# Order of the last three Strassen products of an FFN output, its residual loads, and the order of the MLA projections behind it

## The chip, the cores and the metric

The kernel runs on one core of a Trainium2 chip. The metric is the device time of one execution in microseconds (us), lower is better. The core's engines are named as the profile names them: PE is TensorE (matrix products into PSUM, with PEld for its weight loads), DVE is VectorE, ACT is ScalarE, POOL is GpSimd and SP is SyncE. Loads and stores are issued from the queues of SP, ACT and POOL.

## The reference, cut to what matters

A backbone of two layers runs over 256 latent tokens and 256 context tokens, width 1024. Layer 0 mixes tokens with an mLSTM, layer 1 with multi-head latent attention (MLA); a gated ConvFFN follows each.

```python
x = _layer_norm(ALPHA * x + ml[2] * yl, ln_g[i, 0], ln_b[i, 0])
f = _conv_ffn(_modulate(x, ml[3], ml[4]), ...)
x = _layer_norm(ALPHA * x + ml[5] * f, ln_g[i, 1], ln_b[i, 1])
# the same for the context xc while need_ctx (layer 0 only)

def _conv_ffn(h, w_in, conv_w, conv_b, w_out):
    gate, up = jnp.split(h @ w_in, 2, axis=-1)
    return (jax.nn.silu(_dwconv(gate, conv_w, conv_b)) * up) @ w_out

def _mla_mixer(hl, hc, ...):            # layer 1
    kc, vc = _mla_kv(hc, w_dkv, kv_norm, w_ukv, None)
    kl, vl = _mla_kv(hl, w_dkv, kv_norm, w_ukv, ang)
    ql = _mla_q(hl, w_dq, q_norm, w_uq, ang)
    # latent queries attend to context and latent keys; then @ w_out
```

The change lies between the product with `w_out` of layer 0's FFN ("fout0", 2816 x 1024) and the MLA's keys, values and queries.

## The kernel before

**Arithmetic.** Every float32 matrix product is made of three products of rounded parts (`mm3`: hi x hi, hi x lo, lo x hi). A weight block of 128 x 1024 goes through three steps: a DMA brings it from `in_ws` into a raw tile, ACT rounds it to the high part (L321), and DVE subtracts for the low part (L324). The last two steps are called the split.

**The weight stream.** `_plan` writes the order of all weight blocks out by hand, and the class `Stream` follows it. `use(key)` hands the next block over and splits ahead, at most `NB` = 3 blocks in the "w" buffers; blocks marked wide go to "u" buffers instead and don't count among the three. Raw tiles come from a ring of slots that changes with the stage (`bufs`, L240 to L252): eleven slots from `yt2` on, seven from `y22` on. A slot is loaded again when its block has been split.

**fout0 as one level of Strassen's scheme.** `w_fout0` (L1350) multiplies the FFN's activations, halves of context rows (g = 0) and latent rows (g = 1), with `w_out` in seven products instead of eight. The first four (`yt2`, `y11`, `yt3`, `yt1`, six blocks each, interleaved) fill all eight PSUM banks, a pair for each product: p6, p1, p7, p5. Their sums go to SBUF (`sums`, as a background generator). Then `y21`, `y22` and `yt4` run one after the other, each into a fresh pair of banks. `add` (L1452) multiplies a finished pair by the gate row, adds it to the residual tile `z` and takes the statistics for the layer norm. The weight of `yt4` is a sum: the weight of `yt2`, stored in `t2d`, is loaded back on SP's queue, and the second addend is added by an accumulating load on POOL's queue (L276, L277). The activations of these three products ("zr", then "fz" after their own split) come back from DRAM in 33 loads on ACT's queue (`operand`, L1359).

**Residuals.** Before, `sums` writes gate x partial sum into each half of `z` and adds the residual row `x1d` by an accumulating DMA on POOL's queue (L1424), eight of 256 KB.

**What follows.** When the context rows are complete (after `y22`) they are normalised (`z_norm`), transposed on PE and modulated (`ctx_T`, through `ln_T`) between the two halves of `yt4`'s tail; then the latent rows. `mla_down` (L1609) makes the down projection of the context (`dkv`), the latent transposes, dkv of the latent rows, and the context's keys (`ukn`) and values (`uv`). `mla` makes the query projection `dq`, the latent keys, the rotary queries and the latent values, then attention. `ln_x` scales the latent rows for the next residual and stores them in `x2d`.

**Order.** DVE, ACT, SP and POOL get their order from a planner that takes instructions in program order as their inputs come ready, with `pin` holding some ACT instructions in program order. Each engine then works through its instructions strictly in that order. PE is held in program order from `yt4` on (`manual_schedule`). Background generators (`bg`) are advanced one step at each `tick`.

Of the kernel before, what the change touches and what calls it, by code (L numbers as in the profile page):

```python
# [55 lines left out]
YTAIL = 3  # L56
# [13 lines left out]
def _plan():  # L70
# [162 lines left out]
class Stream:  # L233


    def __init__(self, k, ids, order, ws):
# [14 lines left out]
        self.bufs.append((keys.index(("y22", 0, 0)), self.bufs[-1][1][:7]))  # L251
# [101 lines left out]
class K:  # L353
# [996 lines left out]
    def w_fout0(self, x1d, ctx_T, lat):  # L1350
# [4 lines left out]
        parts = [("2", i) for i in range(6)] + [("S4", i) for i in range(6)] + [("3", i) for i in range(6)]  # L1355
# [20 lines left out]
        def prod(ps, x, w, i, bs=(0, 1)):  # L1376
            for h in range(2 if i < 5 else 1):
                j = 2 * i + h
                a = A[x, j]
                for b in bs:  # L1380
                    ts = slice(b * 128, (b + 1) * 128)
                    cs = slice(h * 512, (h + 1) * 512)
                    self.mm3(ps[b], (a[:, 0, ts], a[:, 1, ts]), (w[0][:, cs], w[1][:, cs]), j == 0, j == 10)
# [7 lines left out]
        u1, u3, u4, vv = [], [], [], []  # L1391
        for i in range(6):
            for name, ps, x in (("yt2", p6, "S2"), ("y11", p1, "1"), ("yt3", p7, "S3"), ("yt1", p5, "S1")):
# [21 lines left out]
        stats = [self.tiny(12, "st").rearrange("p (a b) -> p a b", b=6) for _ in range(4)]  # L1415
        z = [self.uf("z") for _ in range(4)]

        def sums():

            def part(us, g, c):  # L1420
                for b in range(2):
                    zz = z[2 * g + b][:, c]
                    nc.vector.tensor_tensor(zz, us[b], gate[g][:, c], op=ALU.mult)
                    nc.gpsimd.dma_start(zz, x1d[2 * g + b][:, c], accum_op=ALU.add)  # L1424
            for b in range(2):
                u = self.s2("u2")
                nc.vector.tensor_tensor(u, p6[b], u1[b], op=ALU.add)
                u4.append(u)
            yield
            part(u1, 0, lo)  # L1430
            yield
            for b in range(2):
                u = self.s2("u3")
                nc.vector.tensor_tensor(u, p7[b], u4[b], op=ALU.add)
                u3.append(u)
            yield
            for b in range(2):
                v = self.s2("v")
                nc.vector.tensor_tensor(v, p5[b], u3[b], op=ALU.subtract)
                vv.append(v)  # L1440
            yield
            for b in range(2):
                nc.vector.tensor_tensor(u4[b], p5[b], u4[b], op=ALU.subtract)
            yield
            part(u4, 0, hi)
            yield
            part(u3, 1, lo)
            yield
            part(vv, 1, hi)
            yield  # L1450

        def add(g, c, ps, bs=(0, 1)):  # L1452
            for b in bs:
                t = self.s2("zp")
                zz = z[2 * g + b][:, c]
                nc.vector.tensor_tensor(t, ps[b], gate[g][:, c], op=ALU.mult)
                nc.vector.tensor_tensor(zz, zz, t, op=ALU.add)
                nc.vector.bn_stats(stats[2 * g + b][:, c.start // 512], zz)

        self.bg.append(sums())  # L1460
        ps = pair()
        for i in range(6):
            w = st.use(("y21", 0, i))
            prod(ps, "2", w, i)
            self.tick(1)
            operand()
        add(0, lo, ps)
        ps = pair()
        for i in range(6):
            w = st.use(("y22", 0, i))  # L1470
            prod(ps, "S4", w, i)
            self.tick(1)
            operand()
        self.drain()
        add(0, hi, ps)
        self.bg = [self.z_norm(z[0:2], stats[0:2])]
        with self.tc.manual_schedule(engines={mybir.EngineType.PE}):
            ps = pair()
            st.limit = [x[0] for x in st.order].index(("ukn", 0, 0))
            for i in range(6 - YTAIL):  # L1480
                w = st.use(("yt4", 0, i))
                prod(ps, "3", w, i)
                self.tick(1)
                for b in range(2):
                    if i == 2:
                        nc.vector.bn_stats(stats[2 + b][:, 1], z[2 + b][:, hi])
            self.drain()
# [483 lines left out]
```

## Time and profile before

| what | value |
|---|---|
| runs | 1403.27, 1405.13, 1408.07 us; median 1405.13 us |
| profiled execution | 1403.4 us, its span from the first to the last instruction |
| PE busy | 1359.0 us (97%) |
| PEld busy | 1143.8 us (82%) |
| DVE busy | 1070.7 us (76%) |
| ACT busy | 699.4 us (50%) |
| POOL busy | 126.5 us (9%) |
| mean granted clock of TensorE | 0.991 |
| DMA | 297.63 MB, mean 212 GB/s |

Busy shares are means over stages with different limits. PE counts as busy while a matmul is in flight, and matmuls overlap, so its loss shows in three places: idle time with what ended it, the granted clock, and the distance between the starts of successive matmuls. An entry like "[11.88 <-DVE w L324]" says that the engine had been idle for 11.88 us and that the instruction of line 324 on DVE, writing tile w, let it go on.

### The profile page before, as it was taken

How to read it: one execution, taken by the hardware profiler on the slowest of the kernel's cores; microseconds unless marked ns; L12 is line 12 of the kernel's file. 1: busy time of each engine (PE TensorE's matmuls, PEld its weight loads, DVE VectorE, ACT ScalarE, POOL GpSimd, SP SyncE). 2: the span in 40 equal slices, each digit the busy share in tenths (PEclk: the TensorE clock that was granted, in tenths of full speed). 3: DMA queues.
4: the chain of work that ended last, by engine and by line, in shares of the span. 5: the costliest groups of instructions: out<-in, count | busy, mean ns of one | idle time of the engine just before them, and what ended most of it. 6: DMA issues, size and time to landing. Idle time of an engine off the chain costs nothing.

```text
span 1403.4 us, 19160 instructions
## 1 busy us (share of the span) xinstructions
PE 1359.0 (97%) x6903; PEld 1143.8 (82%) x6903; DVE 1070.7 (76%) x1718; ACT 699.4 (50%) x1179; POOL 126.5 (9%) x219
## 2 busy tenths in 40 slices
PE   7999999999999999999999999999968899999997
PEld 3788888888788888878888888888747788999986
DVE  6599756687688697698799887669858789777773
ACT  6585444445544535374553433334527467455560
POOL 0032000010011001110011000000030001000000
PEclk9999999999999999999999999999989999999999
DMA  9689848788665364676747877547894425357650
GB/s 336 222 291 327 282 161 249 238 289 277 212 222 189 109 237 158 202 224 199 260 153 262 278 226 236 168 147 268 257 246 160 149 84 198 125 188 227 209 187 30
DMA packets 98479, 297.63 MB, mean 212 GB/s; under 512 B 12200, under 2 KB 24872, under 8 KB 98384
## 3 DMA queue, kind: packets, MB, share of 16 engines
q1 hardware_dynamic: 68672, 218.52, 47.1%
q0 software_dynamic: 18048, 57.57, 13.5%
q10 hardware_dynamic: 11664, 20.32, 4.0%
q8 instruction: 54, 0.88, 0.3%
q14 instruction: 41, 0.34, 0.1%
HBM read 262.90 MB, written 33.46 MB: 211 GB/s over the span
## 4 chain that ended last, share of the span: by engine, by line
PE 88%; DVE 4%; DMA 3%; ACT 2%; issue 1%; SPq 0%; ACTq 0%; DVEq 0%; POOLq 0%
PE fin L381 9%; PE fin L383 9%; PE fin L382 9%; PE tok L381 6%; PE tok L383 6%; PE tok L382 6%; PE y L382 5%; PE y L383 5%; PE y L381 4%; PE qk L381 4%; PE qk L383 4%; PE qk L382 4%; PE up L381 2%; PE up L383 2%; PE up L382 2%; DMA raw<-in_ws 2%
## 5 line engine op out<-in xcount | busy, mean ns | idle before, releaser
L324 DVE TENSOR_TENSOR w<-raw,w 128x1024 fp32r<-128x1024 f32 (+3 forms) x290 | 348.1, 1203 | 163.0 <-ACT w L321 162.2
L321 ACT CAST w<-raw 128x1024 fp32r<-128x1024 f32 (+3 forms) x290 | 300.3, 1037 | 329.1 <-PE fin L383 106.4
L382 PE MATMUL fin<-h,w 128*128 128x256 f32 (+1 forms) x696 | 231.7, 333 | 0.0
L383 PE MATMUL fin<-h,w 128*128 128x256 f32 (+1 forms) x696 | 231.4, 333 | 0.0
L381 PE MATMUL fin<-h,w 128*128 128x256 f32 (+1 forms) x696 | 231.2, 333 | 0.1
L510 DVE SCALAR_TENSOR_TENSOR junk<-ar,bc 128x1024 f32<-128x1024 f32 x128 | 156.0, 1218 | 4.7 <-ACT bc L552 2.4
L382 PEld LDWEIGHTS fin<-h,w 128*128 128x128 f32 x696 | 132.2, 190 | 13.1 <-DVE h L1210 0.2
L383 PEld LDWEIGHTS fin<-h,w 128*128 128x128 f32 x696 | 132.2, 190 | 12.9
L381 PEld LDWEIGHTS fin<-h,w 128*128 128x128 f32 x696 | 131.9, 190 | 12.9 <-ACT h L1209 0.3
L381 PE MATMUL qk<-xc,w 128*128 128x512 f32 x256 | 100.7, 393 | 0.0
L383 PE MATMUL qk<-xc,w 128*128 128x512 f32 x256 | 99.9, 390 | 0.0
L382 PE MATMUL qk<-xc,w 128*128 128x512 f32 x256 | 99.8, 390 | 0.0
L381 PEld LDWEIGHTS qk<-xc,w 128*128 128x128 f32 x256 | 48.1, 188 | 10.1 <-issue 0.4
L383 PEld LDWEIGHTS qk<-xc,w 128*128 128x128 f32 x256 | 48.1, 188 | 10.0
L382 PEld LDWEIGHTS qk<-xc,w 128*128 128x128 f32 x256 | 48.1, 188 | 9.6
L381 PE MATMUL up<-hT,w 128*128 128x512 f32 x128 | 50.5, 394 | 0.4 <-ACT hT L386 0.3
L382 PE MATMUL up<-hT,w 128*128 128x512 f32 x128 | 50.2, 392 | 0.5 <-DVE hT L387 0.5
L383 PE MATMUL up<-hT,w 128*128 128x512 f32 x128 | 50.1, 391 | 0.3 <-DVE w L387 0.3
L381 PE MATMUL tok<-w,hT 128*128 128x512 f32 x128 | 49.8, 389 | 0.0
L382 PE MATMUL tok<-w,hT 128*128 128x512 f32 x128 | 49.8, 389 | 0.0
L383 PE MATMUL tok<-w,hT 128*128 128x512 f32 x128 | 49.8, 389 | 0.0
L321 ACT CAST wu<-raw 128x1024 fp32r<-128x1024 f32 (+1 forms) x33 | 33.7, 1039 | 23.7 <-DMA raw<-in_ws 23.7
(451 smaller groups left out, 3049.5 us busy)
## 6 DMA issues: line engine op xcount, KB each, us to landing
raw<-in_ws SPq DMA_DIRECT2D x287, 512.0 KB, 4.4
ar<-in_adaT SPq DMA_DIRECT2D x80, 512.0 KB, 4.8
adaw<-in_ada_w SPq DMA_DIRECT2D x32, 256.0 KB, 6.5
t2d<-raw ACTq DMA_DIRECT2D x13, 512.0 KB, 4.6
raw<-t2d SPq DMA_DIRECT2D x13, 512.0 KB, 7.2
raw<-in_ws POOLq DMA_DIRECT2D x13, 512.0 KB, 8.9
zr<-fd ACTq DMA_DIRECT2D x33, 128.0 KB, 4.4
xmd<-xr POOLq DMA_DIRECT2D x16, 256.0 KB, 5.2
```

The lines of the kernel that those rows point to most:

```text
L321: k.nc.scalar.copy(h[:, :cols], src)
L324: k.nc.vector.tensor_sub(l[:, :cols], src, h[:, :cols])
L381: mm(out, w[0], x[0], start=start, stop=False)
L382: mm(out, w[0], x[1], start=False, stop=False)
L383: mm(out, w[1], x[0], start=False, stop=stop)
L510: nc.vector.scalar_tensor_tensor(o, w, 1.0, self.bc[j], op0=ALU.mult, op1=ALU.mult, accum_out=col[:, k, j:j + 1])
```

## The change

1. The last three products run in another order: two blocks of `y21`, all of `yt4`, the rest of `y21`, then `y22`. The latent rows are complete after `yt4`, the context rows after `y22`. The ring of raw slots keeps eleven slots until `yt4` has been loaded.
2. Each of the three accumulates onto a bank pair that is already live: `y21` onto p1, `yt4` onto p7 (into which ACT first copies u3 = p7 + t), `y22` onto p5 (from which t has been subtracted), where t = p6 + u1.
3. The residual rows `x1d` are loaded into `z` by four plain DMAs during the first four products; every `add` then multiplies, adds and takes statistics.
4. Latent rows are normalised and transposed (`lat_T`) between the products of `y22`. PE is held in program order for all three products.
5. `mla_down` runs dkv of the latent rows, then `dq`, then the context transposes, the latent keys and dkv of the context. The context's keys and values come in `mla`, after the rotary queries. The blocks of `dq` come right behind those of `dkv` in the stream and are wide.
6. Keys of two heads share a tile pair and are split once per full PSUM bank.

```diff
-YTAIL = 3
+YTURN = 2
+YLAST = ([("y21", j) for j in range(YTURN)] + [("yt4", j) for j in range(6)] +
+         [("y21", j) for j in range(YTURN, 6)] + [("y22", j) for j in range(6)])
 ...
-    for n in ("y21", "y22", "yt4"):
-        for j in range(6):
-            add((n, 0, j), cols[j], n == "yt4" and j >= 6 - YTAIL)
+    for n, j in YLAST:
+        add((n, 0, j), cols[j])
     for c, m in enumerate((3, 3, 2)):
         add(("dkv", 0, c), m * 320)
+    for c in range(4):
+        add(("dq", 0, c), 768, True)
 ...
-    for c in range(4):
-        add(("dq", 0, c), 768)
 ...
-        self.bufs.append((keys.index(("y22", 0, 0)), self.bufs[-1][1][:7]))
+        self.bufs.append((keys.index(("y21", 0, YTURN)), self.bufs[-1][1][:7]))
 ...
-                if n == 14:
-                    gate = []
-                    for g in (1, 0):
-                        t = self.uf("gate")
-                        nc.gpsimd.dma_start(t, self.gd[0, 5][g:g + 1, :].to_broadcast([128, 1024]))
-                        gate.append(t)
+                if n in (14, 18):
+                    g = 1 - len(gate)
+                    r = self.uf("gate")
+                    nc.gpsimd.dma_start(r, self.gd[0, 5][1 - g:2 - g, :].to_broadcast([128, 1024]))
+                    gate.append(r)
+                    for b in range(2):
+                        z[2 * g + b] = self.uf("z")
+                        nc.gpsimd.dma_start(z[2 * g + b], x1d[2 * g + b])
                 n += 1
                 if (name, i) == ("y11", 5):
                     for b in range(2):
                         u = self.s2("u1")
                         pin(nc.scalar.copy(u, p1[b]))
-                        u1.append(u)
+                        r = self.s2("u2")
+                        nc.vector.tensor_tensor(r, p6[b], u, op=ALU.add)
+                        t.append(r)
+                if (name, i) == ("yt3", 5):
+                    u3 = []
+                    for b in range(2):
+                        r = self.s2("u3")
+                        nc.vector.tensor_tensor(r, p7[b], t[b], op=ALU.add)
+                        nc.scalar.copy(p7[b], r)
+                        u3.append(r)
 ...
-        def sums():
-            def part(us, g, c):
-                for b in range(2):
-                    zz = z[2 * g + b][:, c]
-                    nc.vector.tensor_tensor(zz, us[b], gate[g][:, c], op=ALU.mult)
-                    nc.gpsimd.dma_start(zz, x1d[2 * g + b][:, c], accum_op=ALU.add)
+        for b in range(2):
+            r = self.s2("v")
+            nc.vector.tensor_tensor(r, p5[b], u3[b], op=ALU.subtract)
+            v.append(r)
 ...
+        def latent():
+            yield from add(1, lo, p7)
+            for _ in self.z_norm(z[2:4], stats[2:4]):
+                pass
+            yield
+            yield
+            yield from lat_T(z[2:4])
+
+        def context():
+            yield from add(0, hi, p5)
+            yield from self.z_norm(z[0:2], stats[0:2])
+
+        st.limit = kv0
+        with self.tc.manual_schedule(engines={mybir.EngineType.PE}):
+            for name, i in YLAST:
+                if (name, i) == ("y21", YTURN):
+                    self.drain()
+                    self.bg = [latent()]
+                w = st.use((name, 0, i))
+                ps, more = {"y21": (p1, True), "yt4": (p7, True), "y22": (p5, True)}[name]
+                prod(ps, names[name], w, i, more)
+                if (name, i) == ("yt4", 0):
+                    for b in range(2):
+                        nc.vector.tensor_tensor(p5[b], p5[b], t[b], op=ALU.subtract)
+                    self.bg = [add(1, hi, v)]
+                self.tick(1)
+                operand()
+                if (name, i) == ("y21", 5):
+                    self.bg.append(add(0, lo, p1))
+            self.drain()
+            self.fa = self.fd = None
+            down(context(), z)
 ...
     def ukn(self, g):
-            u = self.kn[h]
-            self.split(u[:, 0, cs], u[:, 1, cs], ps[:, hs])
+            if h % 2:
+                u, v = self.kn[h // 2]
+                self.split(u[:, g], v[:, g], ps)
 ...
+    def mla_down(self, hl, hc, context, ctx_T):
+        wd = [st.use(("dkv", 0, c), hold=True) for c in range(3)]
 ...
+        rows = self.dkv_mm(hl, wd)
+        for _ in context:
+            pass
+        rows = self.dkv_rows(rows, 2)
 ...          # the dq products, as before in mla
+        st.pump(kv0 + 4)
+        self.dkv_T(rows, 2)
 ...          # row norms of dq; wk, wv
+        ctx_T()
+        self.ukn(1)
+        rows = self.dkv_mm(hc, wd)
+        st.unhold("dkv")
+        self.rows = self.dkv_rows(rows, 0)
 ...
     def mla(self):
+        self.uv((2, 3))
 ...          # dq's transposes, rotary query products
         self.drain()
-        self.uv((2, 3))
+        self.dkv_T(self.rows, 0)
+        self.ukn(0)
+        self.uv((0, 1))
```

More of the change, by code (lines that the diff above doesn't have):

```diff
@@ L1348, in act_sums, with w_fout0 @@
         self.fd.append(d)
-    def w_fout0(self, x1d, ctx_T, lat):
+    def w_fout0(self, x1d, kv0, lat_T, down):
         nc, st, A = self.nc, self.st, self.fa
         pin = self.tc.keep_in_program_order
-        parts = [("2", i) for i in range(6)] + [("S4", i) for i in range(6)] + [("3", i) for i in range(6)]
+        names = {"y21": "2", "yt4": "3", "y22": "S4"}
+        parts = [(names[n], i) for n, i in YLAST]
         off = {"2": 0, "3": 256, "S4": 512}
@@ L1390, in w_fout0 @@
         n = 0
[L1391 removed]
+        t, v = [], []
+        z, gate = [None] * 4, []
         for i in range(6):
@@ L1458, in add @@
                 nc.vector.bn_stats(stats[2 * g + b][:, c.start // 512], zz)
[L1460 to L1487, printed above, removed]
-            ws = [(i, st.use(("yt4", 0, i), hold=True)) for i in range(6 - YTAIL, 6)]
-            for b in range(2):
-                for i, w in ws:
-                    prod(ps, "3", w, i, (b,))
-                add(1, lo, ps, (b,))
-                if b == 0:
-                    ctx_T(z[0:2])
-            st.unhold("yt4")
-            self.fa = self.fd = None
+                yield
@@ L1897, in build, with lat_T, down, ctx_T @@
         hc, hl = half(hcu), half(hlu)
-        def ctx_T(zs):
+        def lat_T(zs):
             k.rope_load()
-            for _ in k.ln_T(zs, *k.ln_mod_cols(1, 1, 0, 1), hc, False):
-                pass
-        def lat(zs):
-            def latent():
-                hlu.extend([k.u("hl") for _ in range(4)])
-                for _ in k.ln_T(zs, *k.ln_mod_cols(1, 1, 0, 0), hl, True):
-                    pass
-            k.mla_down(hc, latent, hl)
-            k.late.append(k.ln_x(1, zs, [x2d[0], x2d[1]]))
-        k.w_fout0(x1d, ctx_T, lat)
+            hlu.extend([k.u("hl") for _ in range(4)])
+            yield from k.ln_T(zs, *k.ln_mod_cols(1, 1, 0, 0), hl, False)
+        def down(context, z):
+            def ctx_T():
+                hcu.extend([k.u("hc") for _ in range(4)])
+                for _ in k.ln_T(z[0:2], *k.ln_mod_cols(1, 1, 0, 1), hc, True):
+                    pass
+            k.mla_down(hl, hc, context, ctx_T)
+            k.late.append(k.ln_x(1, z[2:4], [x2d[0], x2d[1]]))
+        k.w_fout0(x1d, kv0, lat_T, down)
         hc = hcu = None
         k.take_late()
-        att = k.mla(hl)
+        att = k.mla()
         oT = next(att)
```

106 lines of the change are left out of this document (36 added, 70 removed).

## The prediction, made before the change was run

> **What bounds the kernel now.** I read the page first, then the span cut into stages, then the waits of TensorE in the stage that the change rewrites, and last the timelines of the engines around its longest wait. The page:
>
> ```profile
> span 1403.4 us, 19160 instructions
> ...
> PEclk9999999999999999999999999999989999999999
> ```
>
> The granted clock leaves the top tenth in one slice, the 30th of 40 (35.1 us each), which lies in the changed stage. The profiled execution takes its span, 1403.4 us; the three timed runs lie between 1403.27 and 1408.07 with median 1405.13. So I work on the profiled span and take the median to be 1.7 us above it, before and after alike. Busy time by stage (columns: stretch, its length, then busy time and count for PE, PEld, DVE, ACT, POOL, then granted clock, DMA share, GB/s):
>
> ```profile
> 941.00:1001.00 60.00, 60.00 (x267) 49.64 (x265) 51.06 (x58) 31.29 (x41) 2.19 (x4) 1.00 0.75 253
> 1001.00:1017.00 16.00, 15.48 (x68) 12.30 (x67) 15.64 (x21) 8.70 (x12) 1.82 (x2) 1.00 0.83 232
> 1017.00:1033.00 16.00, 14.88 (x66) 12.02 (x65) 12.43 (x17) 4.92 (x6) 7.08 (x8) 1.00 1.02 247
> 1033.00:1060.00 27.00, 14.99 (x55) 11.42 (x53) 14.14 (x20) 8.90 (x11) 3.53 (x4) 0.75 0.92 239
> 1060.00:1086.00 26.00, 22.84 (x149) 21.07 (x149) 21.31 (x57) 21.78 (x51) 2.25 (x4) 1.00 0.41 136
> 1086.00:1100.00 14.00, 9.35 (x52) 8.07 (x53) 10.92 (x30) 5.00 (x14) 0.31 (x1) 0.88 0.55 178
> 1100.00:1131.00 31.00, 30.24 (x173) 27.24 (x172) 22.04 (x41) 16.06 (x33) 1.87 (x4) 1.00 0.39 135
> ```
>
> The first row is the four paired products (yt2, y11, yt3, yt1): TensorE never idles there. The next three hold y21, y22 and yt4, the last three the MLA projections up to the first query product. TensorE's idle time is length minus busy: 0.5, 1.1, 12.0, 3.2, 4.7 and 0.8, together 22.2 us. No more than this and some clock is there to be won. TensorE's waits in the six stages after 1001 (us in all, times, the longest):
>
> ```profile
> PE y L382 <- DVE w L324: 13.5, 3, 11.9
> PE kn L381 <- DVE kn L387: 3.8, 4, 1.1
> PE kn L381 <- ACT ckT L1574: 1.8, 2, 1.0
> PE zT L1197 <- DVE z L1512: 1.7, 2, 0.9
> PE kn L382 <- DVE ckT L1575: 0.5, 1, 0.5
> PE dkv L383 <- DVE hl L1210: 0.4, 1, 0.4
> PE dkv L381 <- ACT hl L1209: 0.4, 1, 0.4
> ```
>
> The longest, 11.9 us, is a wait for the split of a yt4 weight on VectorE. What VectorE did then, and TensorE after it:
>
> ```profile
> 1027.74 1.82 DVE L324 TENSOR_TENSOR w<-raw,w 128x1024 fp32r<-128x1024 f32 x2
> 1043.93 0.69 DVE L1486 BATCH_NORM_STATS2 st<-z 128x6 f32<-128x512 f32 x1 [14.37 <-DMA z<-x1d]
> 1044.54 1.21 DVE L324 TENSOR_TENSOR w<-raw,w 128x1024 fp32r<-128x1024 f32 x1
> ```
> ```profile
> 1045.80 0.79 PE L382 MATMUL y<-w,fz 128*128 128x512 f32 x1 [11.88 <-DVE w L324]
> 1046.39 0.63 PE L383 MATMUL y<-w,fz 128*128 128x512 f32 x1
> ...
> 1050.66 0.58 PE L381 MATMUL y<-w,fz 128*128 128x512 f32 x1
> 1051.08 0.39 PE L382 MATMUL y<-w,fz 128*128 128x512 f32 x1
> 1051.31 0.39 PE L383 MATMUL y<-w,fz 128*128 128x512 f32 x1
> ```
>
> So the weight was not what came last. VectorE stood 14.4 us at the statistics of a residual half that an accumulating DMA (z<-x1d) had still to add to, and the weight's split was queued behind. Afterwards ten starts take 4.27 us (0.43 each) until the clock is back, then 0.23: twelve matmuls lost 0.2 us each, 2.4 us. The DMAs of 1001 to 1060 (median us from issue to landing at the end):
>
> ```profile
> raw<-t2d SPq DMA_DIRECT2D x5, 512.0 KB, 9.3
> raw<-in_ws POOLq DMA_DIRECT2D x5, 512.0 KB, 11.9
> z<-x1d POOLq DMA_DIRECT2D x8, 256.0 KB, 12.4
> ```
>
> **The change, part by part.** *Residuals.* Eight accumulating loads of 256 KB go, and with them the statistics' wait: minus 11.9 and minus 2.4 us of clock. In their place stand four plain loads of 512 KB, issued on the POOL queue at products 14 and 18 of the first stage, next to the two gate loads. The gates are the nearest row for them, and the operand loads (zr) are what shares the queues there:
>
> ```profile
> zr<-fd ACTq DMA_DIRECT2D x33, 128.0 KB, 4.4
> ...
> gate<-gd POOLq DMA_DIRECT2D x2, 512.0 KB, 5.6
> ```
>
> At 5.6 us each they land some 20 us before first use, so nothing waits for them. The Trainium skill would price this otherwise: its page "DMA: Bandwidth & Descriptors", section "Anatomy of one DMA — SWDGE (gpsimd) path", fits 2.0 us plus bytes over 436 GB/s, an estimated 2.6 us for 256 KB, at which the accumulating loads would have hindered nobody. The trace's 12.4 us disagrees, and the measurement decides; what the sum would be by that rule stands among the rivals.
>
> What would be late next is yt4 itself: reloaded from t2d on SP, then added to by an accumulating load on POOL. At the medians above that is 21.2 us. yt4's first weight is now the 27th of the order instead of the 37th, inside the ring of eleven raw slots, so it is requested at product 13, thirteen products ahead. A product is twelve starts of 0.23, 2.7 us, four of the thirteen are halves: 30 us, less 2 for the slot's last reader. 28 exceeds 21.2, without the residuals in the queue. How fast accumulation runs, and what it does to others, a stretch shows in which it had the chip:
>
> ```profile
> q0 software_dynamic: 333, 0.97, 103.4%
> q1 hardware_dynamic: 2, 0.00, 0.2%
> ```
>
> This is 1023 to 1029, POOL's queue against SP's: 0.97 MB in 6 us, so 3.2 us for 512 KB and 18 us for the five and a half of yt4; the last lands about when its split is due. SP's loads issued meanwhile moved two packets. Those 18 us now run beside the end of the first stage, whose DMA share is already 0.75, and beside the zr loads on ACT's queue. Their casts stand in program order among ACT's weight casts:
>
> ```profile
> 997.61 0.62 ACT L1371 CAST fz<-zr 128x512 fp32r<-128x512 f32 x1 [1.00 <-DMA zr<-fd]
> ...
> 1000.13 1.06 ACT L321 CAST w<-raw 128x1024 fp32r<-128x1024 f32 x1
> ```
>
> Already now ACT waits 1.0 us for a zr, and the weight cast behind it ends 0.05 us before y21 wants it. A zr pair is requested two products ahead: 5.4 us, but 2.7 us in the last four half products. One accumulation of 3.2 us in front of it delays the casts of perhaps two pairs, less the two split weights in hand: I take 3.0 us, between 0 (ACT's queue shares evenly) and 15 (18 us of accumulation, all but 3 of it felt).
>
> *Product order and live banks.* The six sums p6+u1, p7+t and p5-u3 move from y21 into the last four half products, where VectorE also splits weights. The rows of a full split, of a key split and of a half-width operation (count, busy us, mean ns):
>
> ```profile
> L324 DVE TENSOR_TENSOR w<-raw,w 128x1024 fp32r<-128x1024 f32 x16 | 19.5, 1216 | 2.7 <-ACT w L321 2.7
> ...
> L387 DVE TENSOR_TENSOR kn<-kn 128x256 fp32r<-128x256 f32 x16 | 6.5, 419 | 3.9 <-ACT kn L386 3.9
> ...
> L1456 DVE TENSOR_TENSOR zp<-y,gate 128x512 f32<-128x512 f32 x6 | 4.0, 679 | 0.0
> ```
>
> Six times 0.68 is 4.1 us more within 5.4 us; VectorE idles 15% of the first stage, and the two split weights ahead cover most. I take 1.0 us, from 0 to 4.1. The seeded banks cost TensorE nothing: as many matmuls, and the ACT copies into p7 have two products, 5.4 us, before yt4 needs them. After them the eight gate multiplications become two more of the add's trios: 24 operations where 28 stood, 2.7 us off VectorE, off the path.
>
> *Latent rows first.* Twelve of the sixteen latent transposes go between y22's products. Before the first lie y21's last four products and one of y22, 12.2 us; adding, statistics and normalisation of two rows need about 6 x 0.68 plus 2 us of small steps, beside five splits of 1.2: 12 us. I take 0.3 us of wait, 0 to 3. The waits of zT (1.7) and the two of dkv for hl (0.4 each) go: minus 2.5.
>
> *MLA order.* Context rows now finish behind the latent dkv and dq products. Their lengths, from starts of today's:
>
> ```profile
> 1067.07 0.30 PE L381 MATMUL dkv<-w,hc 128*128 128x320 f32 x1
> ...
> 1074.11 1.91 PE L1197 MATMUL zT<-ident,z 128*128 128x128 f32 x16
> ```
> ```profile
> 1104.54 0.33 PE L381 MATMUL dq<-w,hl 128*128 128x384 f32 x1
> ...
> 1112.89 0.82 PE L1570 MATMUL ckT<-ident,ckr 128*128 128x128 f32 x6
> ```
>
> 7.0 and 8.4, together 15.4 us of cover, against 4.1 for the add, about 4.6 for dq and dkv splits, 2 for the normalisation and 2 for the row norms on VectorE: 12.7, so it holds, with little to spare. If the cover is short, each missing us is one of TensorE. The sixteen key splits become eight over full banks, so TensorE no longer waits for VectorE to read the first half of the bank it writes: minus 3.8, and with it the low clock of that stretch (9.35 us at 0.88, 1.1 us). Here the clock falls after gaps of 1.1 us at most. The Trainium skill's page "TensorE: Matmul & The Clock Gate", section "Part 1: The HAM clock gate", has the clock fall only after an idle window of about 3.4 us; by it these 1.1 us would stay and the gain be smaller by as much. The trace's 0.88 speaks against that. Transposes of context rows now stand between the ckT transposes and the first keys and fill most of kn's waits for ckT (1.8 and 0.5): minus 1.5 of 2.3. Against this, VectorE's work, 96.5 us in the six stages, is squeezed from 130 us into some 113: I take 1.5 us of new waits, 0 to 8. The residual's scaling (eight operations of 0.68, 5.4 us, four loads and four stores on POOL) moves from beside dq to the drain ahead of the context's transposes. Queued behind it on VectorE are the ckT splits that ukn(0) needs; ready value products cover most: 0.5 us, 0 to 5.4.
>
> **Sum.** Off: 11.9 + 2.4 + 2.5 + 3.8 + 1.1 + 1.5 = 23.2. On: 3.0 + 1.0 + 0.3 + 1.5 + 0.5 = 6.3. Net minus 16.9: 1386.5 on the profiled span, 1388.2 as a median.
>
> **Rivals.** *VectorE becomes the bound.* It is at 15.64 of 16 us in the stage after 1001. If splits come late throughout, its terms stand at their upper ends (4.1, 3, 8, 5.4 for 3.3): on is 23.5 with zr's 3.0, the net about 0, 1405; halfway 1397. For: the density; against: a 97% stage now costs 0.5 us. *Slower: ACT stands at zr.* If a pair takes L to land and is asked for two products ahead, ten products from 14 on last L/2 each, against 6 x 2.7 + 4 x 1.36 = 21.6 us. To lose the 19.9 us that are otherwise won, and 4.2 more, L must pass 9.1 us; today it is 4.4. At the 12.4 us of loads behind accumulation the loss is 40 us: about 1425. For: SP's two packets in 6 us; against: accumulation is 18 us in all, and this case takes ten products at 9.1 / 2, 46 us of it. *The wait was not the residuals'*, as by the rule's 2.6 us, or the z tiles find no free slot and load late: 14.3 of the 23.2 stay, net minus 2.6, 1402.5. Against it stands the 14.37 us wait, ended by that very DMA.
>
> **How the numbers follow.** Forecast 0.70; VectorE 0.13, of it half way mostly; zr 0.12; the last 0.05. Something of 0.3%, 4.2 us, is about what a measurement of this kernel can tell from no change. Faster: 0.70 + 0.13 = 0.83; same: 0.05; slower: 0.12. The range's low end is all idle time and clock won, 25.7 off 1405.1: 1379. Its high end, 1400, takes in VectorE's half way case and zr up to 15; above lie zr's case, the last and the tail of VectorE's.
>
> **What would show it.** No row of statistics waiting for z<-x1d; yt4's accumulating loads landing before 1018; every slice of the clock at 9; kn's wait for kn gone; DVE w waits under 3 us together. Step zr is wrong if the operand cast's wait for zr grows past 5 us in all, the projections' step if TensorE idles over 4 us between y22's end and the queries. The forecast falls if y's wait for w stays above 10 us.

## The result, and the profile after

| kernel | median | lowest to highest | ratio to before, 95% interval |
|---|---|---|---|
| before | 1405.14 us | 1403.27 to 1410.52 | |
| changed | 1410.99 us | 1407.69 to 1413.01 | 1.003, 1.0015 to 1.0044 |

The change made the kernel slower by 0.3% where 1.2% faster was forecast. Median and direction both miss, and what came is the rival called slower, though at a smaller price. The profiled execution of the changed kernel took 1407.69 us for a span of 1405.8. A gap of this size stands in every run that was profiled after the change (1.7 to 2.1 us), so it is no difference between runs. The profiled execution is the fastest of the eight: its span is 2.4 us longer than that of before, while the medians differ by 5.9. What the slower executions lost besides, the trace cannot show.

The page of the changed kernel, and the span in the stretches of before (same columns). TensorE idles 0.9 us in the first, then 12.5, 3.0, 0, 2.4, 3.7 and 3.5; the last stretches do not hold quite the same work, since the first query product (tile qn) starts at 1133.62 instead of 1130.86:

```profile
span 1405.8 us, 19141 instructions
...
PEclk9999999999999999999999999999899999999999
```
```profile
941.00:1001.00 60.00, 59.10 (x261) 48.52 (x259) 48.56 (x54) 27.31 (x34) 6.25 (x9) 1.00 0.76 245
1001.00:1017.00 16.00, 3.53 (x12) 2.06 (x11) 4.35 (x7) 5.26 (x9) 3.38 (x5) 0.74 1.06 274
1017.00:1033.00 16.00, 13.04 (x51) 9.77 (x51) 11.92 (x17) 7.58 (x11) 0.00 (x0) 0.94 0.85 287
1033.00:1060.00 27.00, 27.00 (x125) 22.38 (x124) 22.00 (x33) 14.70 (x21) 0.00 (x0) 1.00 0.60 182
1060.00:1086.00 26.00, 23.56 (x136) 21.62 (x134) 21.66 (x37) 15.54 (x28) 0.00 (x0) 1.00 0.59 182
1086.00:1100.00 14.00, 10.28 (x70) 9.95 (x71) 12.60 (x40) 10.58 (x32) 2.20 (x4) 0.76 0.62 188
1100.00:1131.00 31.00, 27.48 (x166) 24.45 (x165) 23.40 (x44) 13.85 (x27) 2.16 (x4) 1.00 0.37 122
```

Two holes have opened. TensorE's waits from 999 to 1134 name them (us in all, times, the longest):

```profile
PE y L1386 <- ACT u L1420: 10.9, 1, 10.9
PE ckT L1550 <- DVE ckr L1503: 5.8, 2, 4.8
PE y L1386 <- DVE w L325: 2.6, 2, 2.3
PE y L1386 <- ACT w L322: 2.5, 2, 1.6
PE kn L383 <- DVE ckT L1555: 2.3, 1, 2.3
PE kn L382 <- ACT ckT L1554: 0.9, 1, 0.9
```

The 11.9 us for the split behind the statistics and the 3.8 us for half key banks are gone, as are the waits for z and hl. In their place TensorE stands 10.9 us at y21's first product, which accumulates onto p1 and so may not start before ACT has copied u1 out of it. What ACT did then, from its timeline, and TensorE after it:

```profile
1003.54 3.39 ACTq L1367 DMA_DIRECT2D zr<-fd  x2
1007.02 1.04 ACT L322 CAST w<-raw 128x1024 fp32r<-128x1024 f32 x1 [4.25 <-DMA zr<-fd]
1007.97 0.92 ACT L1373 CAST fz<-zr 128x256 fp32r<-128x256 f32 x2
1014.23 0.62 ACT L1373 CAST fz<-zr 128x512 fp32r<-128x512 f32 x1 [5.34 <-DMA zr<-fd]
...
1014.75 0.58 ACT L1420 COPY u<-y 128x512 f32<-128x512 f32 x1
```
```profile
1015.38 7.41 PE L1386 MATMUL y<-w,fz 128*128 128x512 f32 x24 [10.90 <-ACT u L1420]
```

The copy needed no data that was late. It stood in ACT's order behind a cast whose zr had not landed. ACT is held in two ways: at the cast (5.34 us), and already at the issue. The two issues starting at 1003.54 span 3.39 us, and the weight cast behind them records 4.25 us of idle time ended by an older zr. What such an issue waits for, the semaphores recorded in the trace say. The loads and stores issued by SP and ACT share eight completion semaphores, and an issue waits until the transfer that had its semaphore before has landed. The second of these two goes out at 1006.60, when the zr asked for at 995.57 has landed (1006.58); that one had gone out when a yt4 reload that SP had issued at 987.16 had landed (995.55). So it is a wait of the program, and through it a late load of either queue holds ACT. Over 941 to 1060 ACT waits at the casts:

```profile
ACT fz L1373 <- DMA zr<-fd: 12.5, 5, 5.3
```

Why zr is late: the DMA issues of 985 to 1030 in the changed kernel (median us to landing), and below them the zr row of the same stretch before:

```profile
raw<-in_ws POOLq DMA_DIRECT2D x5, 512.0 KB, 14.4
...
z<-x1d POOLq DMA_DIRECT2D x4, 512.0 KB, 14.0
zr<-fd ACTq DMA_DIRECT2D x14, 128.0 KB, 13.7
gate<-gd POOLq DMA_DIRECT2D x2, 512.0 KB, 14.3
```
```profile
zr<-fd ACTq DMA_DIRECT2D x14, 128.0 KB, 3.6
```

A load of 128 KB takes 13.7 us instead of 3.6. POOL's own timeline shows the company it is in, first and last issues:

```profile
986.55 0.93 POOL L278 DMA_DIRECT2D raw<-in_ws  x1 [37.26 <-DMA zr<-fd]
987.52 0.56 POOL L1411 DMA_DIRECT2D gate<-gd  x1
...
1010.12 0.86 POOL L278 DMA_DIRECT2D raw<-in_ws  x1 [6.43 <-DMA raw<-t2d]
1010.67 1.41 POOL L1415 DMA_DIRECT2D z<-x1d  x2
```

Eleven and a half loads of 512 KB go out from 986.55; the last z, issued by 1012.1 and 14.0 us from landing at the median, lands at about 1026. That is 39.5 us, 3.4 us for each as a mean over plain and accumulating ones. POOL had stood 37.26 us at the first of them, an accumulating load of yt4, with the gates and z behind it in its order. Without the accumulating loads (after_noacc, below) the gates and z go out between 949 and 974. So the new order brought the plain loads into this stretch too.

The second hole is VectorE's. From its timeline after y22 ends at 1067.3, and TensorE's wait behind it:

```profile
1068.62 1.28 DVE L1442 TENSOR_TENSOR zp<-y,gate 128x512 f32<-128x512 f32 x2
...
1073.61 3.56 DVE L325 TENSOR_TENSOR wu<-raw,wu 128x768 fp32r<-128x768 f32 x4
...
1077.83 1.29 DVE L1442 TENSOR_TENSOR zp<-y,gate 128x512 f32<-128x512 f32 x2
...
1081.54 1.18 DVE L325 TENSOR_TENSOR wu<-raw,wu 128x1024 fp32r<-128x1024 f32 x1
...
1085.63 1.21 DVE L325 TENSOR_TENSOR wu<-raw,wu 128x1024 fp32r<-128x1024 f32 x1
...
1088.24 0.48 DVE L1503 TENSOR_SCALAR ckr<-dkv,rs 128x256 f32<-128x256 f32 x1
```
```profile
1088.78 0.47 PE L1550 MATMUL ckT<-ident,ckr 128*128 128x128 f32 x1 [4.83 <-DVE ckr L1503]
```

The row norms of the latent dkv product, which TensorE finished at 1075.6, are taken at 1088.24, behind both halves of the context's add (from y21 at 1068.62, from y22 at 1077.83), its normalisation and four splits of the ukn and uv blocks.

### The profile page after: what moved, and what is told of

The parts are those of the page before. It is cut to its first block, busy times and chain, and to the rows that moved or that the text cites. A ratio compares the mean times of both kernels' runs of the same rounds, so it can differ in the third digit from the quotient of the medians.

```text
span 1405.8 us, 19141 instructions
## 1 busy us (share of the span) xinstructions
PE 1356.3 (96%) x6903; PEld 1141.3 (81%) x6903; DVE 1068.4 (76%) x1706; ACT 697.7 (50%) x1173; POOL 121.2 (9%) x215
## 4 chain that ended last, share of the span: by engine, by line
PE 87%; DMA 5%; DVE 4%; ACT 2%; issue 1%; SPq 0%; ACTq 0%; DVEq 0%
PE fin L382 9%; PE fin L383 9%; PE fin L384 9%; PE tok L382 6%; PE tok L383 6%; PE tok L384 6%; PE y L1386 5%; PE qk L382 4%; PE qk L384 4%; PE qk L383 4%; PE y L383 3%; PE y L384 3%; PE y L382 3%; DMA zr<-fd 2%; PE up L382 2%; PE up L384 2%
## 5 line engine op out<-in xcount | busy, mean ns | idle before, releaser
L325 DVE TENSOR_TENSOR w<-raw,w 128x1024 fp32r<-128x1024 f32 (+1 forms) x289 | 347.8, 1206 | 181.1 <-ACT w L322 175.0
L322 ACT CAST w<-raw 128x1024 fp32r<-128x1024 f32 (+1 forms) x289 | 299.5, 1037 | 337.4 <-PE fin L384 105.2
L384 PEld LDWEIGHTS fin<-h,w 128*128 128x128 f32 x696 | 132.2, 190 | 12.7
L1386 PE MATMUL y<-w,fz 128*128 128x512 f32 x198 | 48.6, 403 | 13.9 <-ACT u L1420 10.9
L1386 PEld LDWEIGHTS y<-w,fz 128*128 128x128 f32 x198 | 37.6, 193 | 23.6 <-ACT u L1420 11.8
L383 PE MATMUL tok<-w,hT 128*128 128x512 f32 x128 | 49.8, 389 | 0.0
L382 PE MATMUL tok<-w,hT 128*128 128x512 f32 x128 | 49.8, 389 | 0.0
```

The source lines that it names most:

```text
L322: k.nc.scalar.copy(h[:, :cols], src)
L325: k.nc.vector.tensor_sub(l[:, :cols], src, h[:, :cols])
L382: mm(out, w[0], x[0], start=start, stop=False)
L383: mm(out, w[0], x[1], start=False, stop=False)
L384: mm(out, w[1], x[0], start=False, stop=stop)
L1386: nc.tensor.matmul(ps[b], a[:, p, ts], w[q][:, cs], start=j == 0 and n == 0 and not more, stop=j == 10 and n == 2, skip_group_check=True)
```

## The experiments

My theory after the result, called "zr" below: yt4's accumulating loads, moved by the new order into the end of the first stage, delay the zr loads; ACT stands at them and everything behind it in ACT's order is late. Rivals: the plain z and gate loads do it; the copy out of the live bank does it whatever the loads do; yt4's weights are late by themselves. For the second hole: VectorE's order, against VectorE being full.

| kernel | median us | ratio to before | 95% interval |
|---|---|---|---|
| before_plain | 1404.08 | 0.9972 | 0.9953 to 0.9991 |
| after_noacc | 1394.08 | 0.9900 | 0.9875 to 0.9926 |
| after_zearly | 1405.96 | 0.9983 | 0.9969 to 0.9997 |
| after_zrearly | 1395.68 | 0.9914 | 0.9883 to 0.9944 |
| after_copyfirst | 1410.88 | 1.0035 | 1.0016 to 1.0054 |
| after_deep | 1410.11 | 1.0020 | 1.0004 to 1.0037 |
| after_sp_deep | 1397.63 | 0.9931 | 0.9916 to 0.9946 |
| after_turn6 | 1399.04 | 0.9946 | 0.9930 to 0.9962 |
| after_mla | 1403.23 | 0.9979 | 0.9964 to 0.9994 |
| zr_mla | 1387.09 | 0.9870 | 0.9851 to 0.9889 |
| zr_all | 1387.36 | 0.9868 | 0.9854 to 0.9882 |
| zr_all_z | 1392.07 | 0.9899 | 0.9885 to 0.9913 |

They were run in three groups, in which the kernel before had medians of 1408.18, 1407.81 and 1405.76, so the ratios are what is compared. Differences to the changed kernel are the difference of the ratios times 1405.

**What delays zr.** First the accumulating loads alone are taken away, so that the weight of yt4 lacks its second addend while TensorE has the same work:

```diff
             k.nc.sync.dma_start(t[:, :cols], k.t2d[key[0][0], key[1], key[2]][:, :cols])
-            k.nc.gpsimd.dma_start(t[:, :cols], self.ws[n, :, :cols], accum_op=ALU.add)
+            if key[0] == "vt4":
+                k.nc.gpsimd.dma_start(t[:, :cols], self.ws[n, :, :cols], accum_op=ALU.add)
```

> The changed kernel without yt4's six accumulating loads on POOL's queue: the reload from t2d on SP stays, so yt4's weight lacks its second addend. Theory 'zr' by accumulation: zr lands in under 7 us again, the 10.9 us wait for the u1 copy falls under 2 us, and the time falls by 14 to 17, to 1394 to 1397. Rival 'plain loads' (gates and z, six of 512 KB on the same queue, do the harm): at most 5 us are gained, 1406 or more. Rival 'live bank' (the copy of u1 stands in the way whatever the loads do): the wait for u stays over 5 us.

Ratio 0.990, 18 us under the changed kernel. The zr row of its 985 to 1030, and all of TensorE's waits for ACT's w up to 1050:

```profile
zr<-fd ACTq DMA_DIRECT2D x16, 128.0 KB, 3.3
```
```profile
PE y L1387 <- ACT w L323: 1.1, 1, 1.1
```

The wait for u1 is gone with the same live banks and the same copies. But here POOL also reached its gates and z before 985, so this run alone does not part the accumulating loads from the plain ones. The next does:

```diff
-                if n in (14, 18):
+                if n in (2, 6):
```

> The changed kernel with its two gate loads and four z loads at products 2 and 6 of the first stage instead of 14 and 18, so that POOL's queue holds only the accumulating loads when zr's last pairs are asked for. Theory 'zr' by accumulation: POOL's queue is full for 18 us instead of 40, zr lands in 8 to 12 us instead of 12 to 19, and about half of the loss goes: 1411 - 7 = 1404. Rival 'plain loads': all of it goes, about 1395. If the time stays at 1411, the z loads had no part in it.

6.6 us better than the changed kernel, 1405.96. With only the accumulating loads in the stretch, zr still takes 7.8 us at the median and ACT waits 13.5 us at the casts there; TensorE waits 10.3 us for ACT's w. The accumulating loads are enough for the mechanism; the plain ones in the same stretch make about a third of the 18 us.

Then the zr loads are moved away from them:

```diff
-                if n >= 6:
+                if n >= 1:
                     operand()
```

> The changed kernel with the zr loads and their casts begun at product 1 of the first stage instead of 6, so that the last is asked for five products earlier, when POOL's queue has just begun with yt4. Theory 'zr': ACT's wait at zr falls from 12.5 us to under 3, the u1 copy comes on time, y21 starts some 12 us earlier; the time falls by 12 to 16, to 1395 to 1399. Rival 'live bank' (a wait for ACT's copy of u1 that zr does not cause): the wait stays above 5 us. Rival 'yt4 late' (with ACT free, yt4's accumulating loads, the last landing at 1022, are what TensorE waits for): y waits 4 to 8 us for w, 1400 to 1405.

0.9914, 16 us better. TensorE's waits for y between 985 and 1060 are down to one, and the stage that stood still runs:

```profile
PE y L1386 <- DVE w L325: 3.1, 1, 3.1
```
```profile
1001.00:1017.00 16.00, 12.90 (x50) 10.15 (x49) 12.20 (x16) 6.93 (x10) 3.38 (x5) 0.89 1.06 281
```

The first query product starts at 1122.53 instead of 1133.62, so the 10.5 us by which the spans of the two profiled executions differ lie in the traced stages; the rest of the 16 is a difference of medians. ACT's wait at the casts over 941 to 1060 falls from 12.5 to 4.4 us, where under 3 was expected. "Live bank" and "yt4 late" are out as the main cause.

Last, the accumulating loads are moved instead of zr, by changing one size:

```diff
-YTURN = 2
+YTURN = 6
```

(with the ring's change and the latent generator put at y22's first block).

> The changed kernel with YTURN = 6: all of y21 first, then yt4, then y22; the ring of raw slots keeps eleven slots until y22. yt4's weights are asked for four products later, 10.9 us, when most of zr has been asked for. Theory 'zr' by accumulation: the 10.9 us wait for u1's copy falls under 4, the time falls by 7 to 13, unless the latent rows, now with six products of y22 to hide in instead of ten, are late: TensorE's waits for z and hl above 2 us. Rival 'plain loads or copies': the wait stays above 8 us.

0.9946, 12 us better. POOL's first accumulating load goes out at 997.23 instead of 986.55, the wait for u1's copy is 2.2 us and zr's median 5.1. But four of the six gate and z loads go out before 972 here, so the plain loads have moved as well. And ACT still waits 12.2 us at the casts in 985 to 1030, 10.2 of it after 1007, behind the copies of u1; TensorE then waits 5.2 us for weights. The order has made the late loads cost less and has not removed them. The latent transposes in y22 were not late: no wait for z or hl above 0.3 us stands in the trace.

**Live bank or ACT's order.** The copies of u1 go ahead of the zr loads and casts of their product:

```diff
+                if (name, i) == ("y11", 5):
+                    ...  # the copies of u1, from below
                 self.tick(1)
                 if n >= 6:
                     operand()
```

> The changed kernel with ACT's copy of u1 placed ahead of the zr loads and casts of its product in ACT's order; nothing else. Theory 'zr': the 10.9 us wait for the copy goes, but ACT still stands at the same zr casts, with the weight casts for y21's second product and on behind them, so the wait turns up again as y waiting for ACT's w, 7 to 11 us; the time falls by 0 to 4, 1407 to 1411. Theory 'live bank': the copy was the obstacle; y waits for u and w under 4 us together in the turn and the time falls by 8 or more, to 1403 or less.

1.0035, no gain. The wait has changed its name, and grown:

```profile
PE y L1386 <- ACT w L322: 16.4, 5, 13.0
```

So the copy was only the first thing behind the blocked engine.

**Casts or issues.** The casts are given five products instead of two:

```diff
-            if len(got) > 2 or not parts and got:
+            if len(got) > 5 or not parts and got:
```

> The changed kernel with the zr loads where they are, but each pair cast five products after it is asked for instead of two. Theory 'zr' (a pair that takes L to land holds ACT when L exceeds the lookahead): five of the last products are 7 to 13 us against an L of 12 to 19, so ACT's wait for zr halves and the time falls by 5 to 12, to 1399 to 1406. Rival 'the loads themselves' (starting them earlier helped in after_zrearly because the DMA load was spread, not because of ACT's order): nothing is gained here, 1409 to 1412.

Here my theory missed: 1.0020, within 1.4 us of the changed kernel. The waits at the casts went, but ACT now stood at the zr issues, which the profile books to the next instruction on ACT. Its timeline and its waits from 985 to 1024:

```profile
992.26 5.06 ACTq L1367 DMA_DIRECT2D zr<-fd  x2
997.41 0.62 ACT L322 CAST w<-raw 128x512 fp32r<-128x512 f32 x1 [4.92 <-DMA raw<-t2d]
```
```profile
ACT w L322 <- DMA raw<-t2d: 10.6, 3, 4.9
ACT fz L1373 <- DMA zr<-fd: 7.4, 1, 7.4
ACT w L322 <- DMA zr<-fd: 3.6, 1, 3.6
```

Two issues take 5.06 us where two usually take about one: the second, at 996.99, had waited for a reload of SP that landed at 996.97. The 7.4 us in the name of a cast are such a wait too. That cast's own zr, asked for at 988.35, had landed by 999.07; the two issues just ahead of it, at 1018.49 and 1021.34, waited for zr loads of 1000.60 and 1004.21 to land. So a longer lookahead of the use alone buys nothing here: the loads are as late as before (13.2 us at the median), and ACT waits for them at later issues. Next the issues are taken off ACT:

```diff
-                    pin(nc.scalar.dma_start(r[:, h * 256:(h + 1) * 256], self.fd[j][:, off[x]:off[x] + 256]))
+                    nc.sync.dma_start(r[:, h * 256:(h + 1) * 256], self.fd[j][:, off[x]:off[x] + 256])
```

> after_deep with the zr loads issued on SP's queue instead of ACT's: their casts still stand in ACT's order, five products after the request. In after_deep the cast's wait fell, but ACT then stood 3 to 5 us at a time at the zr issues themselves, each waiting for an earlier load to land. Theory 'issues': ACT is held by the issues as much as by the casts; here only the casts are left and the time falls by 5 to 10 from 1410, to 1400 to 1405. Rival 'the loads' latency alone': SP, which issues the weights too, now stands at the same waits, the weights come late, and the time stays within 3 us of 1410 or rises.

0.9931: 12.5 us better than after_deep, more than the 5 to 10 expected. TensorE's waits for u1 and for ACT's w are 1.2 and 1.7 us. But the run changes the time of the loads along with their queue. No longer held in program order, thirty of the 33 were issued by 975.5, where after_deep had issued fourteen. Only three are left in 985 to 1030, 17.3 us at the median, and one of them holds a cast on ACT for 7.1 us. How much of the gain is the other queue and how much the earlier request stays open; that ACT is held at its issues rests on the trace of after_deep.

**The second hole.** Three moves in the projections:

```diff
-        for _ in context:
-            pass
         rows = self.dkv_rows(rows, 2)
+        for _ in context:
+            pass
...
-        st.pump(kv0 + 4)
         self.dkv_T(rows, 2)
+        st.pump(kv0 + 4)
...
-        self.drain()
         self.dkv_T(self.rows, 0)
+        self.drain()
```

> The changed kernel with three things moved in the order of its projections: the row norms of the latent dkv ahead of the context's add and normalisation, the split of the four ukn and uv blocks behind the transposes of the latent dkv rows, and the context's ckT transposes and splits ahead of the draining of the residual's scaling. Theory 'VectorE's order': the waits for ckr (5.8 us) and for ckT (3.1 us) fall under 2 us together and the time falls by 4 to 8, to 1403 to 1407. Rival 'VectorE is full there': the same 22 us of work stand in another order, the wait moves to z (the context's transposes) or to wu, and the time falls by under 2.

0.9979, 7.2 us better. ckr is gone from TensorE's waits after 1060, and kn's wait for VectorE's ckT too; the context's z has come up instead, at a third of the price:

```profile
PE zT L1198 <- DVE z L1492: 1.7, 1, 1.7
PE kn L382 <- ACT ckT L1554: 0.9, 1, 0.9
PE zT L1198 <- PE ckT L1550: 0.7, 1, 0.7
```

The work is the same, so it was the order and not the amount. Which of the three moves did how much was not tried.

**Together.** zr from product 1 and the projections' order:

> The changed kernel with the zr loads begun at product 1 and with the projections' order of after_mla. If the two losses are separate, their gains add: after_zrearly stands 16 us under the changed kernel, another 4 to 8 come off, 1387 to 1392, which is the time that had been forecast. If VectorE is full behind y22 whatever its order, it stays within 2 us of after_zrearly, about 1394 to 1396.

0.9870, a median of 1387.09. The two gains add (16.3 and 7.2 make 23.5; 22.5 measured), and the first query product starts at 1114.95, 15.9 us earlier than before. TensorE's two largest waits from 999 to 1134:

```profile
PE y L1386 <- DVE w L325: 4.1, 1, 4.1
PE zT L1198 <- DVE z L1492: 1.6, 1, 1.6
```

Two more try to take the rest. zr_all asks for two pairs at four products:

```diff
+                if n in (6, 8, 10, 12):
+                    operand()
```

> zr_mla with two zr pairs instead of one asked for at products 6, 8, 10 and 12, so that all have been asked for by product 13, before POOL's queue begins with yt4. In zr_mla ACT still waits 11 us for zr and reloads at the end of the first stage and TensorE 4.1 us for y21's weight, with a granted clock of 0.80 behind it. Theory 'zr': these go, 4 to 6 us less than zr_mla's 1387, and a ratio to before of 0.981 to 0.985. Rival 'yt4 behind it': with ACT free, the accumulating loads of yt4 become the last, y waits 3 to 6 us for w a few products later, and the time is that of zr_mla within 2 us.

0.9868, the same as zr_mla. The rival was right. ACT hardly waits for zr after 985, and what comes last there is yt4's own accumulating load:

```profile
ACT w L322 <- DMA raw<-in_ws: 12.3, 4, 4.9
```

The DMAs are at 1.06 of their time in 1001 to 1017, which suggests, but does not show, that this is close to what the transfers allow in this order. With the gates and z in front of zr's second half:

```diff
-                if n in (14, 18):
+                if n in (8, 12):
```

> zr_all with the gates and z loaded at products 8 and 12 instead of 14 and 18, ahead of yt4's accumulating loads. If these loads only push yt4's loads back in POOL's queue, whatever wait for yt4's weights zr_all has left shrinks, 0 to 3 us. If they delay the zr loads in their new place, ACT waits for zr again and it is 1 to 4 us slower than zr_all.

0.9899, 4.4 us worse than zr_all: zr is late again, ACT waits 10.6 us at the casts over 941 to 1060 (4.1 in zr_all), and TensorE idles 5.2 us of 941 to 1001, against 1.5 in zr_all. All but 0.2 of the 10.6 lie before 985, and the first accumulating load goes out at 995.16. So plain loads on POOL's queue delay zr too.

**The residual's part alone, in the old order.** Plain loads of z at products 14 and 18 of the kernel before:

```diff
-                    nc.vector.tensor_tensor(zz, us[b], gate[g][:, c], op=ALU.mult)
-                    nc.gpsimd.dma_start(zz, x1d[2 * g + b][:, c], accum_op=ALU.add)
+                    r = self.s2("zp")
+                    nc.vector.tensor_tensor(r, us[b], gate[g][:, c], op=ALU.mult)
+                    nc.vector.tensor_tensor(zz, zz, r, op=ALU.add)
```

> One part of the change alone: the kernel before, with the residual rows loaded plainly into z by four POOL loads at products 14 and 18 of the first stage; the sums multiply and add on VectorE instead of an accumulating DMA. Nothing else is changed; yt4's accumulating loads stay behind y22. Theory 'zr' (after lost its gain because the zr loads on ACT's queue stand behind yt4's accumulating loads, which the new product order puts into the first stage): the plain loads alone do little harm, the 11.9 us wait for the yt4 split and its 2.4 us of clock go, 1405 - 14 = about 1391. Rival 'plain loads' (the gates and the 2 MB of z alone delay zr): ACT stands at zr here too by over 5 us, and the time is above 1396. Rival 'yt4' (yt4's weights were late by themselves): the y wait for w keeps over 8 us, 1403 or more.

0.9972: 4 us, not 14. The statistics' wait is gone, but two others stood behind it. VectorE is busy for all of 1017 to 1033 (eight more additions), and the last yt4 blocks, requested no earlier than before, are late by themselves. TensorE's and ACT's waits of 1001 to 1060:

```profile
1017.00:1033.00 16.00, 12.84 (x50) 10.22 (x49) 16.00 (x25) 4.68 (x5) 2.65 (x3) 0.85 0.93 229
```
```profile
PE y L382 <- DVE w L324: 4.6, 3, 3.2
PE y L381 <- ACT w L321: 3.4, 2, 3.0
```
```profile
ACT wu L321 <- DMA raw<-in_ws: 8.7, 2, 7.6
ACT fz L1371 <- DMA zr<-fd: 2.8, 2, 2.1
```

How the 10 us divide between a full VectorE, yt4's loads and the clock at 0.85 was not taken apart further. Of the rivals, 'yt4' fits best: the waits for w are 8.0 us together, at the edge of its 8, and the median lies above 1403. The signs named for 'plain loads' came too: over 941 to 1060 ACT waits 8.1 us at zr, against 1.8 before. But TensorE idles only 1.1 us of 941 to 1001 beside it. The plain loads went out between 950 and 973 here, so this run says nothing of them in the stretch where the changed kernel had them.

## Why the prediction was wrong, step by step

*What came off was sized rightly, for the new order.* The waits for the yt4 split (11.9), for half key banks (3.8), for zT and hl (2.5) are absent from the changed trace, and with the two new holes mended zr_mla has a median of 1387.09 against the forecast 1388.2. But the 14.3 us are not the plain loads' own: alone they bring 4. The rest came only with the new order. That it is yt4's earlier request and the lighter VectorE is read from the waits left in before_plain, and was not tested.

*The zr step failed.* It took 3.0 us, with bounds of 0 and 15, and was to be wrong if the cast's wait passed 5 us. The wait is 12.5 us; asking for zr earlier returns 16.3 us in the median, and 10.5 between the two profiled executions. Its parts failed as follows. The load's latency was taken from the median before, 4.4 us, plus one accumulation of 3.2; it was 13.7. POOL's queue was taken as 18 us of accumulation, with gates and z costed apart as loads that "nothing waits for"; they stand in the same queue, behind yt4's first load, and make it 39.5 us. And the casts alone were counted, not ACT's issues: in the changed kernel 6.85 us of ACT's idle time (the 4.25, and 2.60 before it) end at issues, beside the 12.5 at the casts; in after_deep, over 985 to 1024, 21.6 us end at issues and none at a cast.

*The rival had the mechanism.* "ACT stands at zr" was given 0.12 with a point of decision at 9.1 us; the trace has 13.7. Its time, 1425 at 12.4 us, was too high. It charged ten products from 14 on, but the loads are late only from POOL's first yt4 load at 986.55 on; the 19 asked for in 941 to 985 took 4.1 us at the median. The argument against it, ten products at half of 9.1 us against 18 us of accumulation, compared with the wrong length: the queue was full for 39.5.

*The projections' step failed.* It was to be wrong above 4 us of idle time from y22's end to the queries; there are 9.7. The cover of 15.4 us was set against 12.7 us of VectorE's work. That left out the four splits of ukn and uv, 4.8 us at 1.2 each, and one half of the context's add, 3.9 us from 1068.62 on. Together it is 21.4 us, 6.0 more than the cover, and TensorE waits 5.8 us for ckr. ln_x ahead of the ckT splits was put at 0.5 us between 0 and 5.4; in after_mla, which moves it, the 2.3 us wait goes. The rival of a VectorE that is full has that place right, but after_mla shows that the order decides.

*The sums p6 + u1, p7 + t and p5 - u3* (1.0 us) are named by no row of TensorE's waits, and the seeded banks by a small one: y's wait for ACT's copy into p7 is 0.4 us. *Latent rows first* (0.3 us) held: no wait for zT before y22's end.

*The clock.* It is not at 9 throughout: a slice is at 8, and 1001 to 1017 and 1086 to 1100 stand at 0.74 and 0.76, where the two holes lie. The Trainium skill's page "TensorE: Matmul & The Clock Gate", section "Part 1: The HAM clock gate", names an idle window of about 3.4 us, and holes of 10.9 and 4.8 us agree with it. Whether gaps of 1 to 2 us cost clock, as the prediction's 1.1 us supposed, stays open: zr_mla has waits of 0.7 and 1.6 us in 1060 to 1086 at 0.93, zr_all the same and one of 1.4 more at 1.00.

Of the other signs: no statistics wait for z<-x1d (right), DVE's w waits under 3 us (2.6, right), kn's wait for kn gone (right), yt4's loads landed before 1018 (wrong: the last, of 256 KB, is issued at 1010.12 and takes 12.4 us).

## What to carry to other kernels

When a change moves transfers to another place, put every transfer of that stretch on one list per queue and ask what the small loads beside them will then take; a latency measured in the old company says nothing of the new. A late load on an engine that also computes is charged twice, at its issue and at its use, and everything pinned behind it is late with it, so such loads are asked for before the crowd comes. Look also at which loads share a completion semaphore: their issues wait for one another, on whichever queue they are, and that is a reason, not tried by itself here, to keep them off an engine that computes. A wait that is removed uncovers the next one: cost the part alone, in its own order, before its gain is booked, and count each instruction that the program calls for in a stretch, splits too, before its cover is said to hold.

## What the runs showed of the hardware that was not expected

- 128 KB loads on ACT's queue went from 3.6 to 13.7 us at the median when POOL's queue held accumulating and plain loads of 512 KB, and to 3.3 us without the accumulating ones and with the plain ones gone by earlier (after_noacc). With the accumulating ones alone it was 7.8 (after_zearly).
- Packets of 4 KB on POOL's queue took 327 ns at the median for accumulating loads (after_zearly, 990 to 1010) and 159 ns for plain ones (the same run, 944 to 958). Whether zr is late through the accumulation as such or through the time that the DMA engines are busy with it was not separated; their share was 1.03 to 1.07 from 990 to 1025 in the changed kernel.
- An issue can hold its engine, by a wait of the program: pairs of issues on ACT spanned 3.0 to 5.1 us, each until an earlier transfer with the same completion semaphore, of SP's or ACT's queue, had landed. SP stood the same way at its weight loads, behind zr (985 to 1024, changed kernel):

```profile
SPq L280 <- DMA zr<-fd: 17.4, 2, 9.8
```

- The eleven and a half loads of 512 KB on POOL's queue took 39.5 us, 3.4 us each on the mean, where I had the accumulating ones at 3.2 and the plain ones as free.
